# Conditions' blocks of an adaLN backbone: VectorE's running sums replaced by matmuls on four column strips of TensorE

## The chip, the cores and the metric

The kernel runs on one core of a Trainium2 chip. The metric is the device time of one execution in microseconds (us). About 0.2% of it, 6 us, can be told from no change.

## The reference

One inference step of a diffusion backbone runs four layers over 128 context tokens and 512 latent tokens of width 1024, all in fp32. The layers differ in their token mixer (SSD, gMLP, S5, neighbourhood attention), and each stands inside the same adaLN frame:

```python
cond_ctx = jax.nn.silu(c_ctx)
cond_lat = jax.nn.silu(c)[:, None, :]
for i in range(4):
    hc, gate_c = adaln(xc, norm_g[i], cond_ctx @ w_mod[i] + b_mod[i])
    hl, gate_l = adaln(xl, norm_g[i], cond_lat @ w_mod[i] + b_mod[i])
    # mixer i on hc and hl, output projection, residual with the gates
```

Only the products `cond @ w_mod[i]` matter here. There are two condition vectors of length 1024, and `w_mod[i]` is 1024 x 3072. The 3072 results (shift, scale and gate, 1024 each) are made in six blocks of 512; a block reads 1024 x 512 fp32 of `w_mod`, 2 MB, as eight k tiles of 128 rows.

## The kernel before

**Matmuls of the layers.** `Net.stream` runs all projections of a stage as one stream on TensorE. A unit is 1024 rows of weights for 128 outputs. Weights come as `raw` (512 KB, SyncE's queue, two buffers) and are split into `whi` and `wlo` (three buffers each) by ScalarE and a DMA of GpSimd's queue that adds in place (in S5's projection by GpSimd). A product is three matmuls per k tile (hi*hi, hi*lo, lo*hi), each over two halves of 320 tokens: 48 matmuls a unit. The stream is cut into slots of six matmuls, eight slots a unit, and other work is hung onto slots.

**Order.** A planner of the language arranges each engine's instructions by its own estimate of time, except on engines named in `manual_schedule`: there they stay as the program writes them. TensorE is named everywhere; VectorE, GpSimd and ScalarE only in parts (the first phase, the ends of the projections, the MLP, S5). Loads on SyncE's queue are placed by the planner, and the queue is in order: a load that waits for its buffer holds the ones behind it.

**Conditions' blocks.** The four blocks that layer 0 needs first are made at the start by `mod_pe`: per k tile one fp32 matmul with the two conditions' columns `cs[:, k, :]` as stationary operand (128 x 2) and the tile of `w_mod` as moving one (128 x 512), all into the same two rows of a PSUM bank; ScalarE copies the two rows, and four small transposes turn them so that features lie on partitions. `mod_b` then adds `b_mod` and makes the scale.

All other blocks are made by `mod_ew`, a generator that is advanced by `tick` at chosen slots of another stage: layer 0's blocks 4 and 5 in the SSD stage, layer 1's blocks 0 to 3 in SSD's output projection (`leave(0, ...)`) and 4 and 5 in the MLP, layer 2's six in the MLP's output projection, layer 3's six in S5's output projection. Each step takes two k tiles (`wm`, 512 KB): VectorE multiplies them with the condition's value on each partition and adds to `wacc` (L437 for the first k tile, L439 for the other seven, for both conditions). After four steps TensorE transposes `wacc` in eight pieces of 128 x 128 (L417), and VectorE adds up over what had been the partitions (`modq`, L418). Loads run two to three tiles ahead.

In an output projection, `use` writes each result onto the residual: `add` (VectorE, L610) and a sum of squares (`ssum`). Before it, VectorE also splits the projection's input into hi and lo (`ylo`, `gyl`, `hlo`; L205). The steps of `mod_ew` come at `MS0 + MD0 * s` (30 + 4.2 s) in SSD's projection and at `MS + MD * s` (6 + 4.6 s) in the others.

Of the kernel before, what the change touches and what calls it, by code (L numbers as in the profile page):

```python
# [7 lines left out]
F32 = mybir.dt.float32  # L8
F32R = mybir.dt.float32r
AF = mybir.ActivationFunctionType  # L10
OP = mybir.AluOpType
AX = mybir.AxisListType
# [7 lines left out]
T = TC + TL  # L20
# [7 lines left out]
SP, RM, GL = (58, 3.6), (4, 5.5), 0  # L28
MS, MD, MB = 6, 4.6, 3
# [28 lines left out]
def f(t):  # L58
    return t.bitcast(F32)
# [58 lines left out]
class Net:  # L118
# [235 lines left out]
    def cond(self):  # L354
        nc, c = self.nc, self.const
        x = c.tile([128, 8, 2], F32, name="condx")
        nc.sync.dma_start(x, self.I["cond"])
        t = c.tile([128, 8, 2], F32, name="condt")
        nc.scalar.activation(t, x, AF.Tanh, scale=0.5)
        nc.vector.tensor_scalar(t, t, 1.0, 0.5, op0=OP.add, op1=OP.mult)  # L360
        self.cs = c.tile([128, 8, 2], F32, name="conds")
        nc.vector.tensor_tensor(self.cs, x, t, op=OP.mult)

    def mod_tiles(self, i):
        c = self.const
# [1 line left out]
        self.mods[i] = (c.tile([128, 8, 2], F32, name=f"modA{i}"), m)  # L367
        return m

    def mod_w(self, i, nb, k, n, p, bufs, tag="wm"):  # L370

        w = p.tile([128, n, 512] if tag == "wm" else [128, 2, T], F32, tag=tag, bufs=bufs, name=self.n("wm"))[:, 0:n, 0:512]
        self.nc.sync.dma_start(w, self.I["w_mod"][i, nb, k // 2, :, k % 2:k % 2 + n])
        return w

    def mod_b(self, i, nb, q):
# [5 lines left out]
        if nb in (2, 3):  # L382
# [2 lines left out]
            nc.vector.scalar_tensor_tensor(a[:, s, :], m[:, 4 * nb:4 * nb + 4, :], 1.0, g[:, :, None].to_broadcast([128, 4, 2]),  # L385
                                           op0=OP.add, op1=OP.mult)

    def mod_pe(self, i, p, blocks=range(6), bufs=4, n=1):

        nc = self.nc  # L390
        for nb in blocks:
            q = self.bank("pmod")
            for k0 in range(0, 8, n):
                w = self.mod_w(i, nb, k0, n, p, bufs)
                for j in range(n):
                    k = k0 + j
                    nc.tensor.matmul(q[:2, :], self.cs[:, k, :], w[:, j, :], start=(k == 0), stop=(k == 7))
            r = p.tile([2, 512], F32, tag="modr", bufs=1, name=self.n("modr"))
            nc.scalar.copy(r, q[:2, :])
            q = self.bank("pmodt")  # L400
            for j in range(4):
                nc.tensor.transpose(q[:, 2 * j:2 * j + 2], r[:, 128 * j:128 * j + 128], self.ident[:2, :2])
            self.mod_b(i, nb, q[:, 0:8].rearrange("p (a b) -> p a b", b=2))
            yield

    def mod_ew(self, i, p, blocks=range(6), bufs=2, tags=("wm", "wacc"), pacc=None):


        nc = self.nc
        e = nc.vector  # L410

        def total(nb, acc):
            q = self.small([128, 4, 2], "modq")
            for c in range(2):
                t = self.bank("pmod")
                for j in range(4):
                    self.nc.tensor.transpose(t[:, 128 * j:128 * j + 128], acc[:, c, 128 * j:128 * j + 128], self.ident)  # L417
                e.tensor_reduce(q[:, :, c], t.rearrange("p (a b) -> p a b", a=4), axis=AX.X, op=OP.add)  # L418
            self.mod_b(i, nb, q)
        todo = [(nb, kb) for nb in blocks for kb in range(4)]  # L420
        load = lambda s: self.mod_w(i, todo[s][0], 2 * todo[s][1], 2, p, bufs, tags[0])
        ws = [load(s) for s in range(bufs - 1)]
        done = None
        for s, (nb, kb) in enumerate(todo):
            w = ws.pop(0)
            if s + bufs - 1 < len(todo):
                ws.append(load(s + bufs - 1))
            if kb == 0:
                acc = (pacc or p).tile([128, 2, 512] if tags[1] == "wacc" else [128, 2, T], F32, tag="s5gx" if pacc else tags[1],
                                       bufs=2 if pacc else 2 if tags[1] == "wacc" else bufs,  # L430
                                       name=self.n("wacc"))[:, :, 0:512]
            for j in range(2):
                k = 2 * kb + j
                for c in range(2):
                    a = self.cs[:, k, c:c + 1]
                    if k == 0:
                        e.tensor_scalar(acc[:, c], w[:, j], a, 0.0, op0=OP.mult, op1=OP.add)  # L437
                    else:
                        e.scalar_tensor_tensor(acc[:, c], w[:, j], a, acc[:, c], op0=OP.mult, op1=OP.add)  # L439
            yield  # L440
            if kb == 1 and done:
                total(*done)
            if kb == 3:
                done = nb, acc
                if pacc:
                    total(*done)
                    done = None
        if done:
            total(*done)
        yield  # L450

    def put_beside(self, *work):
# [139 lines left out]
    def leave(self, i, y, sq=None, perm=None, mod=None):  # L592


        nc = self.nc
# [3 lines left out]
        put = lambda s, g: at.setdefault(s, []).append(g)  # L599
# [5 lines left out]
        n = self.layers.index(i) + 1  # L605
# [52 lines left out]
        if i + 1 in self.layers:  # L658
            self.mod_tiles(i + 1)
            blocks = range(4 if i == 0 else 6)  # L660
            self.rest = i == 0
            self.put_beside(self.mod_ew(i + 1, self.tp, blocks, bufs=4 if mod else MB, tags=mod or ("wm", "wacc")))
            for s in range(4 * len(blocks) + 4):
                put((MS0 if i == 0 else MS) + int((MD0 if i == 0 else MD) * s), lambda: self.tick(1))
        self.wlo = nc.gpsimd
# [63 lines left out]
    def put(self, yd, k, y):  # L729

        self.nc.sync.dma_start(yd[:, 2 * k:2 * k + 2, :], y)
# [406 lines left out]
class Mlp:  # L1138
# [30 lines left out]
    def groups(self, N, h, G, tab):  # L1169
        W = N.I["w_mlp"]  # L1170
        jobs, at = [], {}
        put = lambda s, f, *a: at.setdefault(s, []).append(lambda: f(*a))
        one = lambda w, f, *a: jobs.append(([W[w]], h, 128, lambda p: f(N, *a, p)))
        for k in range(16):
            one(16 + k, self.value, G[k // 2], k)
        stats = self.stats(N)
        put(128 + 6, next, stats, None)
        put(128 + 14, next, stats, None)
        for g, P in enumerate(G):
            for j in range(2):  # L1180
                one(2 * g + j, self.input, P, "u", j, AF.Gelu_apprx_tanh)
            for j in range(2):
                one(32 + 2 * g + j, self.input, P, "z", j, AF.Silu)
            t = 128 + 32 * g
            put(t + 14, self.norm, N, P)
            put(t + 22, self.turn, N, P)
            put(t + 27, self.mix, N, P)
            for j, (a, b) in enumerate(CLOSE):
                put(t + a, self.gate, N, P, j)
                put(t + b, self.close, N, P, j)  # L1190
        for s in range(7, 128 + 32 * 8, 8):
            put(s, N.tick, 1)
        if N.rest:

            mod = []
            put(RM[0] - 1, lambda: mod.append(N.mod_ew(1, self.tp, (4, 5), MB, pacc=N.tp)))
            for k in range(10):
                put(RM[0] + int(RM[1] * k), lambda: next(mod[0], None))
        if 2 in N.layers:
            gen = tab.tables(N)  # L1200
            for k in range(90):
                put(SP[0] + int(SP[1] * k), next, gen, None)
        N.play(jobs, at, after=[N.I["w_out"][1, 0, 0]], also=(mybir.EngineType.DVE, mybir.EngineType.Pool))
# [95 lines left out]
class S5tab:  # L1299
# [49 lines left out]
    def load(self, N, tp):  # L1349
        nc, I = N.nc, N.I  # L1350
        lp = tp.tile([128, 3, 128], F32, name="lp")
        nc.sync.dma_start(lp, I["s5_lp"])
        lq = tp.tile([128, 3, 256], F32, name="lq")
        nc.sync.dma_start(lq, I["s5_lq"])
        sgn = tp.tile([128, 8], F32, name="sgn")
        nc.sync.dma_start(sgn, I["s5_sgn"])
        self.given = lp, lq, sgn
# [769 lines left out]
for _name, _w in (("b_mod", 96), ("norm_g", 32), ("final_g", 8), ("dt_bias", 1), ("a_log", 1), ("conv_w", 160),  # L2127
# [1 line left out]
                  ("s5_d", 16), ("b_glu", 16)):  # L2129
    VEC[_name] = (NVEC, _w)  # L2130
    NVEC += _w
NCONST = 664


def net(ctx, tc, I, O, layers=(0, 1, 2, 3)):
# [53 lines left out]
def layout(inp):  # L2189
    a = {k: np.asarray(v) for k, v in inp.items()}  # L2190
    x = np.concatenate([a["x_prompt"][0], a["x_sample"][0]], 0).T
    r = {"x": np.ascontiguousarray(x.reshape(8, 128, T).transpose(1, 0, 2))}
    r["cond"] = np.ascontiguousarray(np.stack([a["c_ctx"], a["c"][0]], 0).reshape(2, 8, 128).transpose(2, 1, 0))
    i = np.arange(128)
    r["consts"] = np.concatenate([i[:, None] == i, i[:, None] % 8 == i[:8],
                                  i[:, None] <= i, i[:, None] >= i, i[:, None] > i, i[:, None] < i,
                                  i[:, None] // 8 == i[:16]], 1).astype(np.float32)
    r["w_mod"] = np.ascontiguousarray(a["w_mod"].reshape(4, 4, 2, 128, 6, 512).transpose(0, 4, 1, 3, 2, 5))
    r["w_out"] = np.stack([tiles(w, 8) for w in a["w_out"]])
    w = a["ssd_w_in"][0]  # L2200
# [38 lines left out]
    c, k, rw = np.arange(16), np.arange(32), np.arange(8)  # L2239
# [10 lines left out]
    w = bias.reshape(16, 2, 128, 3, 256).transpose(0, 2, 1, 3, 4)  # L2250
# [43 lines left out]
```

## Time and profile before

| what | value |
|---|---|
| median of 3 runs | 3027.43 us (3025.84 to 3032.1) |
| the profiled execution's own time | 3024.37 us |
| its span, first to last instruction | 3022.4 us |
| busy: TensorE, VectorE, ScalarE, GpSimd | 2747.4, 2085.6, 1478.1, 1275.1 us |
| VectorE's L439, `wacc` | 280 instructions, 224.7 us |
| `w_mod` loads | 96 of 512 KB |

PE is TensorE's matmuls, PEld its weight loads, DVE VectorE, ACT ScalarE, POOL GpSimd, SP SyncE; a `q` behind the name is the engine's queue. Busy times count overlapping instructions once. An fp32 matmul leaves two records, one of the fp32r type (the layers' streams) one. A record's duration holds some 0.2 us of latency that the next one overlaps, so the rate of a stream is read from many records in a stretch, not from the mean of one.

### The profile page before, as it was taken

Reading aid. Unit: us, or ns where it says so; the run is one execution under the profiler, and the core shown is the slowest. Engines: PE = TensorE matmul, PEld = TensorE weight load, DVE = VectorE, ACT = ScalarE, POOL = GpSimd, SP = SyncE. Lnnn points to the kernel's source line nnn. Section 1 sums busy time; section 2 is a strip of 40 time slices with the busy share of each in tenths; the row PEclk is TensorE's granted clock in tenths of the full one; section 3 lists DMA queues with packets and bytes.
Section 4 is the critical chain, followed back from the end, with each engine's and each line's share of the span. In section 5 each row is a group of like instructions: output and inputs, shape, how many; then the busy total and the mean of one; then the engine's idle time right before and its main releaser. Section 6 shows DMA issues by size and latency. Waiting matters only on the chain.

```text
span 3022.4 us, 50482 instructions
## 1 busy us (share of the span) xinstructions
PE 2747.4 (91%) x18412; PEld 2636.6 (87%) x18412; DVE 2085.6 (69%) x4948; ACT 1478.1 (49%) x2525; POOL 1275.1 (42%) x1452
## 2 busy tenths in 40 slices
PE   6879989999988888989898876999899999999998
PEld 3768989899988888989898775999889999999998
DVE  5987776676679887735888972225957777777842
ACT  5534434534443444356675553444136666666641
POOL 4466667512576663123443540223343333333332
PEclk9989999999999999999898887999999999999999
DMA  7666667797676667967676569324525444444342
GB/s 254 170 182 164 174 164 192 191 288 220 172 215 194 164 194 227 278 184 219 164 221 169 147 172 186 106 92 135 202 86 148 133 135 131 136 129 135 111 181 85
DMA packets 271734, 517.91 MB, mean 171 GB/s; under 512 B 77888, under 2 KB 146944, under 8 KB 270464
## 3 DMA queue, kind: packets, MB, share of 16 engines
q1 hardware_dynamic: 240512, 411.93, 44.5%
q0 software_dynamic: 24064, 87.04, 14.9%
q10 hardware_dynamic: 6912, 15.73, 1.4%
q8 instruction: 146, 2.39, 0.3%
q14 instruction: 100, 0.82, 0.1%
HBM read 333.83 MB, written 65.70 MB: 132 GB/s over the span
## 4 chain that ended last, share of the span: by engine, by line
PE 31%; DVE 25%; DMA 13%; POOL 9%; ACT 8%; issue 7%; SPq 1%; ACTq 0%; POOLq 0%; DVEq 0%
PE acc L326 25%; DMA wlo<-raw 4%; DVE S L1771 3%; DVE wacc L439 2%; DVE sl L1768 2%; DVE e L2077 2%; DVE cacc L915 2%; POOL dd L1022 2%; POOL dd L1029 2%; ACT e L2075 1%; DMA raw<-in_w_mlp_dram 1%; DVE sb L2072 1%; DMA raw<-in_w_out_dram 1%; DVE pt L205 1%; DVE yn L2108 1%
## 5 line engine op out<-in xcount | busy, mean ns | idle before, releaser
L326 PE MATMUL acc<-hhi,whi 128*128 128x320 f32 (+2 forms) x3472 | 624.2, 319 | 25.4 <-DVE x L610 10.2
L326 PE MATMUL acc<-hlo,whi 128*128 128x320 f32 (+2 forms) x3472 | 633.0, 319 | 2.5 <-DVE hlo L579 1.3
L326 PE MATMUL acc<-hhi,wlo 128*128 128x320 f32 (+2 forms) x3472 | 613.9, 318 | 6.8 <-DMA wlo<-raw 6.8
L326 PEld LDWEIGHTS acc<-hhi,whi 128*128 128x128 f32 (+1 forms) x3472 | 542.7, 193 | 35.3 <-issue 14.6
L326 PEld LDWEIGHTS acc<-hhi,wlo 128*128 128x128 f32 (+1 forms) x3472 | 544.8, 194 | 13.2 <-DMA wlo<-raw 8.7
L326 PEld LDWEIGHTS acc<-hlo,whi 128*128 128x128 f32 (+1 forms) x3472 | 544.7, 193 | 7.9 <-DVE hlo L579 2.8
L226 POOL DMA_DIRECT2D wlo<-raw x164 | 145.1, 891 | 541.8 <-ACT wlo L225 491.9
L205 POOL TENSOR_TENSOR wlo<-raw,whi 128x1024 fp32r<-128x1024 f32 x95 | 244.6, 2576 | 262.9 <-ACT whi L204 86.7
L227 ACT CAST whi<-raw 128x1024 fp32r<-128x1024 f32 (+1 forms) x164 | 170.6, 1041 | 244.8 <-DMA raw<-in_w_mlp_dram 100.3
L225 ACT ACTIVATE wlo<-raw 128x1024 fp32r<-128x1024 f32 (+1 forms) x164 | 173.2, 1057 | 168.7 <-DMA raw<-in_w_mlp_dram 87.9
L439 DVE SCALAR_TENSOR_TENSOR wacc<-wm,conds,wacc 128x512 f32<-128x512 f32 x280 | 224.7, 855 | 30.4 <-DMA wm<-in_w_mod_dram 30.4
L326 PE MATMUL acc<-y,whi 128*128 128x320 f32 (+2 forms) x1024 | 175.8, 312 | 7.1 <-DVE y L746 3.1
L1771 DVE TENSOR_TENSOR S<-S,sl 128x32 f32<-128x32 f32 x1008 | 176.4, 230 | 0.0
L204 ACT CAST whi<-raw 128x1024 fp32r<-128x1024 f32 x125 | 129.2, 1046 | 76.0 <-PE acc L326 67.8
L326 PEld LDWEIGHTS acc<-y,whi 128*128 128x128 f32 x1024 | 155.5, 188 | 10.6 <-DVE y L746 4.5
L2077 DVE TENSOR_SCALAR e<-e,mx 128x384 f32<-128x384 f32 (+1 forms) x160 | 154.1, 963 | 4.2
L915 DVE SCALAR_TENSOR_TENSOR cacc<-pad,vec,cacc 128x644 f32<-128x644 f32 x128 | 144.2, 1127 | 2.2 <-ACT cacc L913 0.9
L2075 ACT ACTIVATE e<-sb,mx 128x384 f32<-128x384 f32 x128 | 79.0, 617 | 107.3 <-DVE mx L2074 106.6
L1768 DVE TENSOR_TENSOR sl<-S,A 128x64 f32<-128x64 f32 x504 | 120.9, 280 | 0.0
L1889 DVE TENSOR_TENSOR y<-y,sg 128x640 f32<-128x640 f32 x16 | 14.1, 879 | 150.2 <-ACT sg L1888 150.2
L1547 POOL TENSOR_TENSOR s5gy<-Bu,Qt 128x512 f32<-128x512 f32 x64 | 90.0, 1438 | 57.3 <-DVE s5gx L1557 53.9
L1022 POOL TENSOR_TENSOR dd<-cmat,dt 128x512 f32<-128x512 f32 x80 | 108.2, 1358 | 12.2 <-DVE dt L826 9.4
(407 smaller groups left out, 5381.9 us busy)
## 6 DMA issues: line engine op xcount, KB each, us to landing
wlo<-raw POOLq DMA_DIRECT2D x163, 512.0 KB, 5.4
wm<-in_w_mod_dram SPq DMA_DIRECT2D x96, 512.0 KB, 6.5
raw<-in_w_out_dram SPq DMA_DIRECT2D x64, 512.0 KB, 4.5
raw<-in_w_nat_dram SPq DMA_DIRECT2D x64, 512.0 KB, 3.8
raw<-in_w_ssd_dram SPq DMA_DIRECT2D x48, 512.0 KB, 3.5
raw<-in_w_mlp_dram SPq DMA_DIRECT2D x48, 512.0 KB, 3.6
fb<-fd SPq DMA_DIRECT2D x40, 512.0 KB, 5.4
s5X<-s5gx SPq DMA_DIRECT2D x32, 512.0 KB, 4.8
```

The lines of the kernel that those rows point to most:

```text
L204: (hi_eng or nc.scalar.copy)(hi, src)
L205: (lo_eng or nc.vector).tensor_tensor(lo, src, f(hi), op=OP.subtract)
L225: self.nc.scalar.activation(lo, raw, AF.Copy, scale=-1.0)
L226: self.nc.gpsimd.dma_start(lo, raw, accum_op=OP.add)
L227: self.nc.scalar.copy(hi, raw)
L326: mm(p[:m, o:o + c], w[:, kt, :], v(hx), start=(k == 0 and wi == 0), stop=(k == 8 * len(units) - 1 and wi == 2))
L439: e.scalar_tensor_tensor(acc[:, c], w[:, j], a, acc[:, c], op0=OP.mult, op1=OP.add)
L915: nc.vector.scalar_tensor_tensor(acc, pad[:, j:j + 644], w(j), acc, op0=OP.mult, op1=OP.add)
L1022: nc.gpsimd.tensor_tensor(dg.rearrange("p (h l) -> p h l", h=4), N.ident[:, None, :].to_broadcast([128, 4, 128]), self.dt[:, c, 32 * d + 4 ...
L1768: e.tensor_tensor(t[d], F[:, d, at[d], None, :].to_broadcast([128, 2, 32]), A[:, :, d], op=OP.mult)
L1771: e.tensor_tensor(dst[d], dst[d], t[d][:, k].rearrange("p (r g) -> p r g", r=2)[:, ::1 - 2 * k], op=OP.add)
L2077: nc.vector.tensor_scalar(e[:, :w], e[:, :w], m[:, 3:4], None, op0=OP.mult)
```

## The change

The eight matmuls of a block are spread over four groups of 32 columns of TensorE: k tile k writes to PSUM partitions 32 (k mod 4) to 32 (k mod 4) + 31, so that four partial sums stand beside each other. The stationary operand is 32 columns wide, starting at the two columns of k (the 30 others are neighbours or zeros and are not used). ScalarE copies the whole bank (128 x 512), and four fp32 matmuls with `sel` (128 x 2, ones where the partition is 0 or 1 modulo 32) add the four partial sums and turn them in one step. `mod_pe` and `mod_ew` both use it; `wacc`, VectorE's sums, the transposes and `modq` go. `mod_ew` is still advanced in four steps per block: all four loads of a block at once, the end of the block before in the second step, the matmuls in the fourth, and then the next block's loads. Buffers: four `wm` tiles instead of two or three and two `wacc`; where only three fit, the fourth is lent by another tag.

```diff
@@ cond
+        self.csx = c.tile([128, 48], F32, name="condsx")
+        nc.vector.memset(self.csx, 0.0)
+        nc.vector.tensor_copy(self.csx[:, 0:16], self.cs.rearrange("p k c -> p (k c)"))
+        self.sel = c.tile([128, 2], F32, name="sel")
+        nc.sync.dma_start(self.sel, self.I["consts"][:, 664:666])
@@ new
+    def mod_sums(self, ws):
+        q = self.bank("pmod")
+        for k, w in enumerate(ws):
+            o = 32 * (k % 4)
+            self.nc.tensor.matmul(q[o:o + 32, :], self.csx[:, 2 * k:2 * k + 32], w, start=(k < 4), stop=(k >= 4))
+        return q
+
+    def mod_end(self, i, nb, r):
+        q = self.bank("pmodt")
+        for j in range(4):
+            self.nc.tensor.matmul(q[:, 2 * j:2 * j + 2], r[:, 128 * j:128 * j + 128], self.sel, start=True, stop=True)
+        self.mod_b(i, nb, q[:, 0:8].rearrange("p (a b) -> p a b", b=2))
@@ mod_pe
+            ws = [self.mod_w(i, nb, k, n, p, bufs) for k in range(0, 8, n)]
+            q = self.mod_sums([w[:, j, :] for w in ws for j in range(n)])
+            r = p.tile([128, 512], F32, tag="modr", bufs=1, name=self.n("modr"))
+            self.nc.scalar.copy(r, q)
+            self.mod_end(i, nb, r)
@@ mod_ew, in place of VectorE's sums
+        lend = lambda: more[0].tile([128, 2, 512], F32, tag=more[1], bufs=2, name=self.n("wm"))
+        load = lambda nb: [self.mod_w(i, nb, 2 * kb, 2, p, MB if more else 4, tags[0], lend if more and kb == 3 else None)
+                           for kb in range(4)]
+        blocks = list(blocks)
+        ws, done = load(blocks[0]), None
+        for n, nb in enumerate(blocks):
             yield
+            if done:
+                self.mod_end(i, *done)
+                done = None
+            yield
+            yield
+            q = self.mod_sums([w[:, j, :] for w in ws for j in range(2)])
...
+            self.nc.scalar.copy(r, q)
+            done = nb, r
+            if n + 1 < len(blocks):
+                ws = load(blocks[n + 1])
+            yield
+        self.mod_end(i, *done)
         yield
@@ leave
-            self.put_beside(self.mod_ew(i + 1, self.tp, blocks, bufs=4 if mod else MB, tags=mod or ("wm", "wacc")))
+            self.put_beside(self.mod_ew(i + 1, self.tp, blocks, tags=mod or ("wm", "modr"), more=(self.tp, "wacc") if i == 1 else None))
@@ groups (the MLP)
-            put(RM[0] - 1, lambda: mod.append(N.mod_ew(1, self.tp, (4, 5), MB, pacc=N.tp)))
+            put(RM[0] - 1, lambda: mod.append(N.mod_ew(1, self.tp, (4, 5), more=(N.tp, "s5gx"))))
@@ constants
-NCONST = 664
+NCONST = 666
```

## Rows read from the trace of the kernel before

**Rows 1.** The page: head, and shares of the chain that ended last, by engine.

```profile
PE 2747.4 (91%) x18412; PEld 2636.6 (87%) x18412; DVE 2085.6 (69%) x4948; ACT 1478.1 (49%) x2525; POOL 1275.1 (42%) x1452
...
PE 31%; DVE 25%; DMA 13%; POOL 9%; ACT 8%; issue 7%; SPq 1%; ACTq 0%; POOLq 0%; DVEq 0%
```

**Rows 2.** Windows of tile `wacc`: length, busy by engine (instructions), clock, DMA, GB/s.

```profile
60.00:200.00 140.00, 0.00 (x0) 0.00 (x0) 29.31 (x32) 0.90 0.65 172
630.00:710.00 80.00, 4.42 (x32) 3.63 (x32) 42.13 (x64) 1.00 0.94 273
735.00:800.00 65.00, 2.35 (x16) 1.77 (x16) 23.21 (x32) 0.95 0.83 229
1175.00:1300.00 125.00, 6.21 (x48) 5.60 (x48) 64.57 (x96) 0.99 0.88 258
2090.00:2200.00 110.00, 4.77 (x32) 4.44 (x32) 86.06 (x96) 0.95 0.56 188
```

**Rows 3.** Windows of all engines, same columns.

```profile
150.00:180.00 30.00, 20.50 (x123) 18.75 (x124) 30.00 (x30) 11.77 (x18) 18.54 (x14) 0.85 0.66 189
630.00:660.00 30.00, 30.00 (x209) 30.00 (x209) 21.25 (x35) 8.12 (x10) 2.59 (x3) 1.00 1.00 310
750.00:780.00 30.00, 29.63 (x204) 29.31 (x204) 26.03 (x38) 13.43 (x19) 9.51 (x7) 1.00 0.85 234
1230.00:1260.00 30.00, 30.00 (x211) 29.98 (x210) 24.28 (x41) 9.41 (x10) 2.64 (x3) 1.00 0.94 271
2125.60:2187.60 62.00, 62.00 (x416) 61.85 (x416) 62.00 (x83) 9.75 (x11) 27.55 (x7) 0.96 0.62 213
```

**Rows 4.** TensorE's waits, 60 to 200 us: for whom, us, times, longest.

```profile
PE G L1054 <- DVE xw L1047: 7.9, 2, 7.3
PE stc L1077 <- DVE xw L1047: 7.1, 1, 7.1
...
PE acc L326 <- DVE hlo L205: 0.5, 1, 0.5
```

**Rows 5.** TensorE's waits, 2090 to 2225 us.

```profile
PE acc L326 <- DVE x L610: 10.2, 3, 6.6
```

**Rows 6.** TensorE's waits, 1175 to 1305 us.

```profile
PE acc L326 <- DVE ylo L205: 2.5, 2, 2.2
```

**Rows 7.** Timeline of TensorE, 33 to 41 us: start us, us, what.

```profile
33.44 7.03 PE L397 MATMUL pmod<-wm,conds 128*2 128x512 f32 x16
```

**Rows 8.** Timeline of TensorE, 212 to 216 us.

```profile
212.30 0.39 PE L1054 MATMUL G<-c,b 128*128 128x128 f32 x2
...
215.25 0.66 PE L1068 MATMUL yd<-dd,xb 128*64 128x128 f32 x8
```

**Rows 9.** Timeline of TensorE, 215.2 to 215.3 us.

```profile
215.25 0.33 PE L1068 MATMUL yd<-dd,xb 128*64 128x128 f32 x2
```

**Rows 10.** Timeline of TensorE's weight loads, 215 to 216.2 us.

```profile
215.25 0.42 PEld L1068 LDWEIGHTS yd<-dd,xb 128*64 128x64 f32 x8 [0.19 <-issue]
```

**Rows 11.** Timeline of TensorE, 655 to 670 us.

```profile
662.17 1.04 PE L417 MATMUL pmod<-cmat,wacc 128*128 128x128 f32 x8
```

**Rows 12.** Timeline of TensorE, 0 to 75 us.

```profile
30.27 1.28 PE L469 MATMUL cols<-ones,ssum 128*128 128x1 f32 x10
```

**Rows 13.** Timeline of ScalarE, 40 to 59 us.

```profile
54.88 1.06 ACT L225 ACTIVATE wlo<-raw 128x1024 fp32r<-128x1024 f32 x1 [11.34 <-DMA raw<-in_w_ssd_dram]
...
56.77 0.57 ACT L399 COPY modr<-pmod 2x512 f32<-2x512 f32 x1
```

**Rows 14.** TensorE's waits, 600 to 735 us.

```profile
PE pmod L417 <- DVE wacc L439: 0.7, 1, 0.7
```

**Rows 15.** Timeline of TensorE, 2190 to 2200 us.

```profile
2190.65 3.77 PE L326 MATMUL acc<-hhi,whi 128*128 128x320 f32 x16 [2.87 <-DVE x L610]
...
2196.95 2.51 PE L326 MATMUL acc<-hhi,wlo 128*128 128x320 f32 x16
```

**Rows 16.** VectorE's waits, 600 to 760 us.

```profile
DVE wacc L439 <- DMA wm<-in_w_mod_dram: 10.5, 6, 3.9
```

More of the change, by code (lines that the diff above doesn't have):

```diff
@@ L368, in mod_tiles, with mod_w @@
         return m
-    def mod_w(self, i, nb, k, n, p, bufs, tag="wm"):
-        w = p.tile([128, n, 512] if tag == "wm" else [128, 2, T], F32, tag=tag, bufs=bufs, name=self.n("wm"))[:, 0:n, 0:512]
+    def mod_w(self, i, nb, k, n, p, bufs, tag="wm", lend=None):
+        w = lend() if lend else p.tile([128, n, 512] if tag == "wm" else [128, 2, T], F32, tag=tag, bufs=bufs, name=self.n("wm"))
+        w = w[:, 0:n, 0:512]
         self.nc.sync.dma_start(w, self.I["w_mod"][i, nb, k // 2, :, k % 2:k % 2 + n])
@@ L388, in mod_pe @@
     def mod_pe(self, i, p, blocks=range(6), bufs=4, n=1):
-        nc = self.nc
         for nb in blocks:
[L392 to L403, printed above, removed]
-            yield
@@ L406, in mod_ew @@
[L406 to L439, printed above, removed]
-            yield
[L441 to L449, printed above, removed]
@@ new lines, in mod_pe, with mod_ew @@
+            ws = [self.mod_w(i, nb, k, n, p, bufs) for k in range(0, 8, n)]
[3 more added lines that the diff above has]
+            self.mod_end(i, nb, r)
+            yield
+    def mod_ew(self, i, p, blocks=range(6), tags=("wm", "modr"), more=None):
+        lend = lambda: more[0].tile([128, 2, 512], F32, tag=more[1], bufs=2, name=self.n("wm"))
[4 more added lines that the diff above has]
+        for n, nb in enumerate(blocks):
+            yield
+            if done:
[4 more added lines that the diff above has]
+            q = self.mod_sums([w[:, j, :] for w in ws for j in range(2)])
+            if more:
+                r = lend()[:, 0]
+            elif tags[1] == "modr":
+                r = p.tile([128, 512], F32, tag="modr", bufs=1, name=self.n("modr"))
+            else:
+                r = p.tile([128, 2, T], F32, tag=tags[1], bufs=4, name=self.n("modr"))[:, 0, 0:512]
+            self.nc.scalar.copy(r, q)
[4 more added lines that the diff above has]
+        self.mod_end(i, *done)
@@ L2196, in layout @@
                                   i[:, None] <= i, i[:, None] >= i, i[:, None] > i, i[:, None] < i,
-                                  i[:, None] // 8 == i[:16]], 1).astype(np.float32)
+                                  i[:, None] // 8 == i[:16], i[:, None] % 32 == i[:2]], 1).astype(np.float32)
     r["w_mod"] = np.ascontiguousarray(a["w_mod"].reshape(4, 4, 2, 128, 6, 512).transpose(0, 4, 1, 3, 2, 5))
```

## The prediction

> **What bounds the kernel now.** The head of the page comes first: TensorE is busy for 91% of the span and VectorE for 69%, yet the chain that ended last gives TensorE 31% and VectorE 25% [rows 1]. So no engine bounds the whole kernel, and what VectorE's sums cost has to be read stage by stage. The windows of the tile `wacc` say where they stand: 29.3 us of VectorE at the start of the SSD stage, 42.1 in SSD's output projection, 23.2 at the start of the MLP, 64.6 in the MLP's projection, 86.1 in S5's projection [rows 2]; 32 instructions are two blocks, so there are 20 blocks.
>
> Next, the busy windows of all engines in the same places show which of these VectorE us are in anybody's way [rows 3]. Where TensorE does only its 320-column matmuls it fits 209 to 211 records into 30 us (630 to 660, 1230 to 1260). There VectorE is busy for 21 to 24 us of 30 and holds nobody up; any work put on TensorE lengthens the stage by its own length. 750 to 780 is nearly such a place (204). It is otherwise at 150 to 180: 123 records, VectorE busy for all 30.0. In S5's projection VectorE is busy for all 62.0 us of the window, while TensorE keeps its rate between waits.
>
> The waits confirm it. From 60 to 200 us, eight kinds of TensorE's waits end on VectorE, from 7.9 us for `xw` down to 0.5 for `hlo`, 26.3 us together [rows 4]. In S5's projection it waits 10.2 us for `x`, the residual update behind the sums in VectorE's queue [rows 5]; in the MLP's, 2.5 us for `ylo` [rows 6].
>
> **The sums on TensorE.** A block's eight fp32 matmuls are 16 records, which took 7.03 us in the first layer, 0.43 each [rows 7]. This is what they cost one after another. The change gives four of them different 32-column strips. No row has four strips, but `yd` has two: it alternates between two strips of 64. Eight of its records, 128 columns each, took 0.66 us from first start to last end, while two records of the untiled `G`, same shape, took 0.39 [rows 8]. With 0.27 us of latency in each, that is 0.12 a record untiled and 0.055 in two strips: the strips run beside each other. The first two `yd` records both start within 50 ns [rows 9], so records of different strips pair up from the first. I take four strips as four times: 7.03 / 4 = 1.76 us. The weight load of `yd` sits idle for 0.19 us at the change of strip width [rows 10], and there is a change back: 0.25 us for both. So 2.0 us a block. The other ends are 3.7 (pairs only) and 7.1 (no overlap).
>
> The Trainium skill, TensorEngine Tiling, Key Properties, says that changing the tiling mode drains TensorE, which speaks against short tiled groups in a dense stream; the 0.19 us agrees, and at twice a block it changes the sum by the 0.25 already in it.
>
> The end of a block stays equal. Eight transposes of 128 x 128 took 1.04 us [rows 11]; now four fp32 matmuls of 128 x 2 run, eight records, nearest to `cols`, ten records in 1.28 us [rows 12], so 1.0 us. ScalarE gets a 128 x 512 copy per block, nearest the 2 x 512 copy of 0.57 us; it is busy for 8 to 9 of 30 us in the projections [rows 3], which hides it. The number of `w_mod` loads stays the same; one small load, of `sel`, joins SyncE's queue at the start.
>
> **Stage by stage.**
>
> Start (0 to 60 us): the first four blocks become 5 us shorter each on TensorE. But block 3's end waits for ScalarE's copy at 56.77, which stands behind two conversions whose raw weights came at 54.88 [rows 13]. The weights' buffer is what is late, not the sums: 0. If ScalarE's order comes out otherwise, at most the 11.3 us that it waited for those weights are saved; if the added small copies and the DMA of `sel` tell, +1. Range -11 to +1.
>
> SSD start: VectorE loses 29.3 us, in a stretch where TensorE waits some 26 us for VectorE. Neither end is likely: VectorE also waits there for a DMA and GpSimd, and those chains stay. I take half, -14.6, and +4.0 for two blocks on TensorE, whose order is fixed as written: -10.6. Range -25 (all returns) to +4 (none).
>
> SSD's projection: 4 blocks x 2.0 = 8.0 on a full TensorE, less a wait of 0.7 for `wacc` there [rows 14]: +7.3. MLP start: two blocks, 4.0, nearly all visible: +3.5. MLP's projection: 6 x 2.0 = 12.0, less the 2.5 us wait: +9.5.
>
> S5's projection: back come the 10.2 us of waits, and slow clock behind them. TensorE restarted at 2190.65 with 16 records in 3.77 us against 2.51 a little later [rows 15]; the window before has a granted clock of 0.96 over 62 us, that is 5 us at 1.2 instead of 2.4 GHz, 2.5 us lost. With 1.4 for the restart at 2190, 14.1 returns; 12.0 is added: -2.1. Range -8 (the projection also gets shorter waits elsewhere) to +8 (VectorE's freedom gives back a third).
>
> Waits for `w_mod`: until now a late tile stopped VectorE (10.5 us in SSD's projection [rows 16]) and not TensorE. Now the sums stand in TensorE's written order, and a late tile stops the stream; all four loads of the next block are issued only after the sums of this one, and SyncE's loads of `w_out` queue behind them. Between two blocks' sums lie 17 or 18 slots of six matmuls, 0.86 us each by the 209 records in 30 us, so 15 us, for 2 MB; the DMA is at 1.00 there and moves 310 GB/s for all [rows 3], so half of that rate would do it in 13 us. Tight, not short: +3 us over the three projections, range 0 to +20.
>
> Sum: 0 - 10.6 + 7.3 + 3.5 + 9.5 - 2.1 + 3 = +10.6 us. The profiled execution took 3024.37 us, 2 us more than its span, and lies 3 us under the median of 3027.43; the sum, made on the trace, is carried to the median: 3038.
>
> **Rivals.**
>
> A, faster: the SSD start returns everything. Place: 60 to 200 us; price: 29.3 instead of 14.6 us, and with prompt loads (no +3) the sum becomes -7, so 3020. For it: VectorE has no idle time at all from 150 to 180. Against: the waits on `fb` and GpSimd. It decides once more than 25 of the 29.3 us return. Chance 0.23.
>
> B, the strips overlap only in pairs. Each fp32 matmul is two records on the same strip; if TensorE starts records strictly in program order, the second must wait for the first, and the next strip can start only then. A block then costs 3.7 us, 1.7 more, on 18 blocks that lie beside full TensorE or fill it: +31, so 3069. Against it stand the first two `yd` records, which start together, where such an order would start the second a whole record later. No overlap at all would be 5 us more on 20 blocks, some 3135. Chance 0.13, with 0.02 of it for the last. The Trainium skill, TensorE: Matmul & The Clock Gate, part 3, states that matmuls start and end in strict program order; by that rule B would be the outcome, and `yd` doesn't bear it out for two strips.
>
> C, the wait for `w_mod` takes the place of the one removed: late tiles stop TensorE for about 1.25 us in each of the projections' 16 blocks: +20 instead of +3, so 3055. For it: the DMA at 1.00 and VectorE's 10.5 us; against: a slower TensorE stream also asks for fewer weights a microsecond. Chance 0.19.
>
> The forecast itself: 0.45.
>
> **How the numbers follow.** About 0.2% (6 us) is what a measurement of this kernel tells from no change. The likeliest case gives 3038, its own range 3028 to 3050 from half of the SSD range and half of the S5 range. Slower by over 0.2%, above 3033.5: three quarters of the forecast's 0.45, all of B and C: 0.66, of which I give 0.07 back for the planner, which orders the engines anew and may do so better. Faster, under 3021.4: most of A and some of that: 0.22. Within: the rest, 0.19. For the range, A's lower half (0.08) is left out below 3017, and half of B (0.08) above 3070.
>
> **What would show it.** `pmod` matmuls with 16 records in about 2.0 us, four starting together, confirm the strips; 3.5 us is B. From 60 to 200 us, `wacc` gone and waits for `xw` cut to half is the forecast; gone altogether is A. In the projections of SSD and the MLP, TensorE's stage gets longer by 7 to 10 us with the record rate unchanged; waits of `pmod` for `w_mod` over 1 us each are C. In S5's projection, the three waits [rows 5] vanish and the stage keeps its length. The step that I trust least is the half at the SSD start, then the 3 us of waits; wrong strips would make all other terms small.

## The result and the profile after

The changed kernel took 3050.7 us (median of four runs, 3048.85 to 3056.26) against 3028.52 for the kernel before on the same chip (four runs, 3025.84 to 3032.10). The ratio is 1.0071, 95% interval 1.0058 to 1.0084, so it is slower by 22 us (18 to 25). Slower was forecast, with 3038 and a range of 3017 to 3070; the loss is twice the 10.6 us of the sum, and 3050.7 lies just above the likeliest case's own range of 3028 to 3050.

The page of the profile after, head and chain (compare [rows 1]):

```profile
span 3054.5 us, 50800 instructions
...
PE 2781.9 (91%) x18748; PEld 2651.1 (87%) x18748; DVE 1832.3 (60%) x4590; ACT 1487.4 (49%) x2543; POOL 1246.1 (41%) x1452
...
PE 39%; DVE 22%; DMA 10%; ACT 8%; POOL 7%; issue 5%; SPq 1%; ACTq 0%; POOLq 0%; DVEq 0%
```

VectorE lost 253 us of work and the kernel got slower: most of that work stood in nobody's way. TensorE got 34 us more, and its share of the chain rose from 31% to 39%.

TensorE's timeline from 640 us, in SSD's projection, and the same cut short at 640.55 (start us, us, what):

```profile
640.50 1.93 PE L400 MATMUL pmod<-wm,condsx 128*32 128x512 f32 x16
```

```profile
640.50 0.64 PE L400 MATMUL pmod<-wm,condsx 128*32 128x512 f32 x4
```

A block is 16 records in 1.93 us, where [rows 7] had 7.03; four of them have started within 50 ns. This is the 2.0 us a block of the prediction.

TensorE's waits from 60 to 200 us (compare [rows 4]), and then in S5's projection, 2120 to 2255 us (compare [rows 5]):

```profile
PE stc L1074 <- DVE xw L1044: 4.7, 2, 3.3
PE G L1051 <- DVE dd L1054: 4.0, 1, 4.0
...
PE st L1074 <- DVE xw L1044: 1.3, 1, 1.3
PE G L1051 <- DVE xw L1044: 0.5, 1, 0.5
```

```profile
PE acc L326 <- DVE x L607: 0.8, 1, 0.8
```

The waits for `xw` fell from 15.0 us and more to 6.5, and one for `dd` came up instead. In S5's projection 10.2 us became 0.8.

Windows of all engines where TensorE is full, and 150 to 180 us, where VectorE held it up before (compare [rows 3]; length, busy by engine with instructions, granted clock, DMA, GB/s):

```profile
630.00:660.00 30.00, 30.00 (x215) 26.99 (x213) 5.50 (x9) 10.85 (x12) 3.48 (x4) 1.00 0.87 234
150.00:180.00 30.00, 30.00 (x215) 28.41 (x214) 20.60 (x24) 14.86 (x24) 18.89 (x18) 1.00 0.60 155
1260.00:1290.00 30.00, 30.00 (x213) 28.37 (x212) 4.15 (x10) 8.78 (x11) 2.61 (x3) 1.00 0.92 256
2155.00:2217.00 62.00, 62.00 (x439) 56.08 (x441) 8.59 (x15) 12.37 (x14) 16.86 (x8) 1.00 0.60 191
```

In the three projections VectorE dropped from between 21 and 62 us busy to under 9, and TensorE is as full as before: these stages can only get longer, by the blocks. From 150 to 180 us TensorE now has 215 records where it had 123.

To see where the 22 us arose, the traces were laid beside the first profile of the kernel before: each instruction of ScalarE and VectorE that occurs equally often in both (the conditions' own left out) was compared with the same occurrence by its start, and the median offset was taken at the ends of the stages. What the offset gains from one end to the next is the table; columns are the ends of the stages in us of the first profile, and all kernels of the experiments are in it. Each row is one execution, and executions differ: the changed kernel's took 3056.26 us, 6 over its median, and the first profile of before 3024.37, 4 under that of before, so the first row adds up to 32 us and not to 22.

```
                        58  355  605  735  935 1174 1324 1775 1925 2288  end
changed kernel        -5.3 -7.3  1.3  9.3 13.3  0.9  8.1  2.0  8.2  2.1 -0.6
before, again          1.0 -1.7 -0.7  0.6  4.1  0.1 -3.0  2.2  0.6  1.2  0.2
before, shifted        0.1 -4.1  2.3  1.1  4.4  0.5 -1.9  3.3  5.9 -1.0  0.2
14 more columns       -5.4 -7.0  0.9  7.1 13.8  1.9  8.2  5.4  6.5  2.0 -0.1
change in place       -4.8 -8.2  0.9  7.3 12.3  2.3  6.6  3.3  3.6  1.7 -0.4
ScalarE's order       -5.4-10.1 -1.6  8.3  4.6  4.6  6.9  4.7  6.5  1.0 -2.6
in place and order    -5.0 -8.9  2.8  7.3  5.0  3.1  6.6  4.9  2.8  1.9 -2.7
not the MLP's start   -4.8 -6.3  2.6  7.1  3.5  1.5  8.6  7.1  9.1  2.3 -0.1
first and SSD start   -4.7-11.0 -1.4  0.0 10.1  4.4 -0.3  3.0  7.9  2.7  0.4
 and S5's projection  -4.6 -7.2  1.6  0.2  8.0  2.7  0.3  5.8  7.7 -0.6  1.4
first and SSD, place  -5.0 -8.7 -0.4 -0.1  6.0  2.4 -0.1  2.6  5.1 -0.6  1.8
 and S5's, in place   -5.6-12.7 -1.4  0.7  4.1  1.9 -3.7  2.9  0.9  1.0  2.2
one strip              0.4 -7.9 -1.8 28.8 17.3  2.4 40.0  0.5  8.6 31.2  0.0
```

Two columns of the first row stand out: 13.3 us at the MLP's start (up to 935), where 3.5 were forecast, and 8.2 at the end of the S5 stage (1775 to 1925), where no instruction came or went. The experiments are about these.

TensorE's waits from 738 to 925 us, before and after (for whom, us, times, longest):

```profile
PE acc L326 <- DMA wlo<-raw: 5.7, 6, 2.5
```

```profile
PE acc L326 <- DMA wlo<-raw: 13.7, 5, 4.7
```

ScalarE's timeline of the changed kernel there, from 784 us (start us, us, what, idle before and releaser), and GpSimd's:

```profile
784.56 1.06 ACT L225 ACTIVATE wlo<-raw 128x1024 fp32r<-128x1024 f32 x1 [4.41 <-DMA raw<-in_w_mlp_dram]
785.53 1.03 ACT L227 CAST whi<-raw 128x1024 fp32r<-128x1024 f32 x1
786.46 0.58 ACT L441 COPY wm<-pmod 128x512 f32<-128x512 f32 x1
790.91 1.05 ACT L227 CAST whi<-raw 128x1024 fp32r<-128x1024 f32 x1 [3.87 <-DMA raw<-in_w_mlp_dram]
791.86 0.70 ACT L1206 ACTIVATE y<-acc 128x640 f32<-128x640 f32 x1
792.46 1.05 ACT L225 ACTIVATE wlo<-raw 128x1024 fp32r<-128x1024 f32 x1
793.40 0.73 ACT L1213 ACTIVATE sq<-y 128x640 f32<-128x640 f32 x1
```

```profile
781.82 0.87 POOL L226 DMA_DIRECT2D wlo<-raw  x1
794.29 1.57 POOL L1214 TENSOR_TENSOR ssum<-ssum,sq 128x640 f32<-128x640 f32 x1 [11.60 <-ACT sq L1213]
795.81 0.87 POOL L226 DMA_DIRECT2D wlo<-raw  x1
```

Read it as a chain. At 784.56 and 785.53 ScalarE starts to write `wlo` and `whi` of one unit. The planner now puts the next unit's `whi` ahead of this unit's `y` and `sq`; it waits 3.87 us for raw weights, and everything behind it waits too. `sq` comes at 793.40, GpSimd's `ssum` stands behind `sq`, and the accumulating DMA that finishes `wlo` stands behind `ssum` in GpSimd's queue: it is issued at 795.81, though `wlo` was written by 785.6. The raw buffer comes free later still, so the next load and TensorE's next units are late.

### The profile page after: what moved, and what is told of

It reads as the page before. It is cut to its first block, busy times and chain, and to the rows that moved or that the text cites. A ratio compares the mean times of both kernels' runs of the same rounds, so it can differ in the third digit from the quotient of the medians.

```text
span 3054.5 us, 50800 instructions
## 1 busy us (share of the span) xinstructions
PE 2781.9 (91%) x18748; PEld 2651.1 (87%) x18748; DVE 1832.3 (60%) x4590; ACT 1487.4 (49%) x2543; POOL 1246.1 (41%) x1452
## 3 DMA queue, kind: packets, MB, share of 16 engines
q0 software_dynamic: 24064, 87.04, 15.2%
## 4 chain that ended last, share of the span: by engine, by line
PE 39%; DVE 22%; DMA 10%; ACT 8%; POOL 7%; issue 5%; SPq 1%; ACTq 0%; POOLq 0%; DVEq 0%
PE acc L326 31%; DVE S L1768 3%; DMA wlo<-raw 3%; DVE sl L1765 2%; DVE e L2074 2%; DMA raw<-in_w_mlp_dram 2%; DVE cacc L912 2%; ACT e L2072 1%; POOL dd L1019 1%; DVE sb L2069 1%; DVE yn L2105 1%; POOL dd L1026 1%; DVE pt L205 1%; ACT zr L1611 1%; PE S L2063 1%
## 5 line engine op out<-in xcount | busy, mean ns | idle before, releaser
L205 POOL TENSOR_TENSOR wlo<-raw,whi 128x1024 fp32r<-128x1024 f32 x95 | 230.1, 2422 | 274.6 <-PE acc L326 105.8
L326 PEld LDWEIGHTS acc<-y,whi 128*128 128x128 f32 x1024 | 156.5, 189 | 12.7 <-DVE y L205 4.1
L607 DVE SCALAR_TENSOR_TENSOR x<-acc,mod,x 128x128 f32<-128x128 f32 (+3 forms) x53 | 29.3, 595 | 224.0 <-PE acc L326 222.6
L2105 DVE TENSOR_TENSOR yn<-yn,av 64x128 f32<-64x128 f32 x320 | 90.6, 283 | 32.4 <-ACT yn L2103 23.6
```

The source lines that it names most:

```text
L205: (lo_eng or nc.vector).tensor_tensor(lo, src, f(hi), op=OP.subtract)
L326: mm(p[:m, o:o + c], w[:, kt, :], v(hx), start=(k == 0 and wi == 0), stop=(k == 8 * len(units) - 1 and wi == 2))
L2105: nc.vector.tensor_tensor(y[r, o], y[r, o], p[r, w:w + 128], op=OP.add)
```

## The experiments

Ten kernels were run 5 to 12 times each; two, the kernel before itself and the one with one strip, once. Times are medians, with the kernel before on the same chip. Single runs of the kernel before spread from 3014 to 3041 us over these sessions, so only ratios with their intervals count.

**ScalarE's order at the MLP's start.**

```
+        act = ExitStack()
+        put(3, lambda: act.enter_context(N.tc.manual_schedule(engines={mybir.EngineType.Activation})))
+        put(57, act.close)
```

> The changed kernel, but at the MLP's start (slots 3 to 57 of its stream) ScalarE takes its work in the order in which it is written (lo half, hi half, y, square), as the planner had it before the change. Theory (the planner's new order, in which a conversion that waits for late weights stands ahead of y and its square, delays the next weights' loads and so TensorE): about 8 us return, +14 us against the kernel before instead of +22; the waits of TensorE for wlo from 755 to 930 fall from 13.7 us to about 6. Rival (the eight w_mod loads that now come in bursts of four are what delays the weights): nothing returns, +22 us, the waits stay above 12 us.

Measured: 3041.2 against 3031.34, ratio 1.0037 (1.0023 to 1.0052): 11 us slower by the ratio, instead of 22. The MLP's start is at +4.6 in the table, and the wait from 738 to 925 us in this kernel is back at

```profile
PE acc L326 <- DMA wlo<-raw: 7.1, 4, 3.3
```

with all 20 blocks still on TensorE. The order it is, and not the bursts of `w_mod` loads, which stayed: SyncE's queue issues four in a row in both traces.

**Two blocks less: the MLP's start on VectorE as before** (`N.mod_ve`, the old `mod_ew`, for blocks 4 and 5 of layer 1).

> The changed kernel, but the two blocks at the MLP's start are summed on VectorE as before. Theory (these two blocks cost 13 us in the profile, 4 of them TensorE's own work): +10 us against the kernel before. Rival (they cost their TensorE time only, and what else was lost from 755 to 930 is another matter): +18 us.

Measured: 3042.86, ratio 1.0042 (1.0025 to 1.0058), 13 us slower: nearer to the theory, and the rival's 18 is just outside the interval. The MLP's start is at +3.5. As the kernel before repeated has +4.1 there, the two blocks cost about 9 us in the changed kernel and next to nothing with ScalarE's order written out. Its row in the table is of an execution of 3055.1 us, the longest of the five.

**Only the first four blocks and the SSD start**; the other 18 blocks by the old `mod_ew`; and the same with S5's projection on TensorE as well.

> TensorE's sums for the first four blocks and the two blocks at the start of the SSD stage alone; the other 18 blocks on VectorE as before. Theory (the gain made there, 4 us in the first 60 us and 6 to 12 at the SSD start, stays to the end): -10 us against the kernel before, range -7 to -14. Rival (it is given back at a later wait): within 3 us of the kernel before.

> As the run with the first blocks and the SSD start alone, and S5's projection too on TensorE (12 of 24 blocks). Theory (there 14 us of waits return and 12 us of TensorE's time are added): the same as that run within 3 us, about -10 us against the kernel before. Rival (the 8 us that the changed kernel's profile shows in the S5 stage between 1780 and 1880 come with the change): 6 to 10 us more than that run, some -2 us.

Measured: 3035.17, ratio 1.0011 (0.9996 to 1.0026), and 3034.8, ratio 1.0019 (1.0006 to 1.0032). The theory fell: 16 us are gained up to 355 us in the one and 12 in the other, as the table shows, and all is gone at the end. The losses lie in stages that these kernels don't change, and every kernel with the change's tiles has about the same loss at the end of the S5 stage. Their largest loss, 10.1 and 8.0, is at the MLP's start, where they have neither the two blocks on TensorE nor the changed order of ScalarE. Either the first profile of before was quick there, or something shared slows them.

**The kernel before, again; and with its buffers shifted.**

```
+        pad = c.tile([128, 50], F32, name="condpad")
+        nc.vector.memset(pad, 0.0)
```

> The kernel before, once more with a profile, since in all five profiles with TensorE's sums the MLP's start (755 to 925) and the S5 stage (1325 to 1900) come out 4 to 13 and 10 to 15 us longer than in the first profile of the kernel before, also where nothing was changed in them. Theory A (these stages wait for transfers whose time differs from execution to execution, and the first profile of before was a quick one): this profile has them 5 to 12 us longer in sum than the first. Theory B (something that all five kernels share makes these stages slower): this profile has them as the first, within 3 us.

> The kernel before with 50 more unused columns (200 bytes a partition, as much as the change's two small constant tiles) in the pool of constants, so that every later buffer lies 200 bytes further on. Theory B, in the form that the shift of the buffers is what all five kernels share: 8 to 12 us slower than the kernel before, in the MLP's start and the S5 stage. Theory A: no change, within 3 us.

The repeated kernel ran in 3028.92 us. Its profile has 4.1 us more at the MLP's start and 2.8 more in the S5 stage than the first: 4 us at the MLP's start can be the spread of executions. The shifted kernel took 3036.11 against 3029.25, ratio 1.0024 (1.0013 to 1.0036): 7 us slower. In the built program each engine has the same instructions in the same order as before, but for that memset, and the same waits, but for one that moved between two loads of `x`. So both theories hold, each for its part, and this shift of the buffers costs 7 us (4 to 11). The end of the S5 stage is at +5.9.

**Another shift.**

```
-        self.csx = c.tile([128, 48], F32, name="condsx")
+        self.csx = c.tile([128, 62], F32, name="condsx")
```

> The changed kernel with 14 more unused columns in its constant tile, so that all later buffers lie 256 bytes instead of 200 further on than before. Theory B (the odd shift slows transfers): some 10 us return, +12 us against the kernel before. Theory A: +22 us as the changed kernel, within 4 us.

Measured: 3052.23, ratio 1.0066 (1.0043 to 1.0089): nothing returned. The run didn't test what it was meant to. In the built program tiles are placed in steps of 32 bytes; `wlo` and `raw` lie on multiples of 256 bytes in the kernel before, 160 bytes past one in the changed kernel, and 224 past one here and in the shifted kernel. No multiple was restored. These places are the built programs'; the traces hold no addresses.

**One strip for all eight k tiles.**

```
-            o = 32 * (k % 4)
+            o = 0
...
-            self.nc.tensor.matmul(q[o:o + 32, :], self.csx[:, 2 * k:2 * k + 32], w, start=(k < 4), stop=(k >= 4))
+            self.nc.tensor.matmul(q[o:o + 32, :], self.csx[:, 2 * k:2 * k + 32], w, start=(k == 0), stop=(k == 7))
```

ScalarE's copy and the four matmuls of `mod_end` take these 32 rows alone.

> The changed kernel with all eight k tiles of a block on the same 32 columns, one after another, so that the sums are the same and no strips lie beside each other. By the trace of the kernel before (0.43 us a record): 7 us a block instead of 2, so +100 us on the 20 blocks that were on VectorE, some 3145 us; the first four blocks longer too, where they are not waiting for data. If the strips gave nothing, the time would stay at 3050.

Measured: 3143.64 us in one run, +93 over the changed kernel, as expected. TensorE's timeline of this kernel from 640 us:

```profile
641.49 7.05 PE L400 MATMUL pmod<-wm,condsx 128*32 128x512 f32 x16
...
664.80 7.05 PE L400 MATMUL pmod<-wm,condsx 128*32 128x512 f32 x16
```

In the table the projections are 19.5, 31.9 and 29.1 us longer than in the changed kernel: 4.9, 5.3 and 4.9 us a block, the 5.1 us between 7.05 and 1.93. There nearly all of TensorE's time is visible.

**The conditions packed in place.** The three small tiles of the conditions (192 bytes) become one, which also serves as `csx` and `sel`:

```
+        self.csx = c.tile([128, 48], F32, name="conds")
+        x, t = (self.csx[:, o:o + 16].rearrange("p (k c) -> p k c", c=2) for o in (0, 16))
+        self.sel = self.csx[:, 46:48]
...
+        nc.vector.tensor_tensor(x, x, t, op=OP.mult)
+        nc.vector.memset(self.csx[:, 16:32], 0.0)
```

> The whole changed kernel, but its padded conditions and its selector lie in the 192 bytes a partition that the three small tiles of the conditions took before. In the built program the later buffers then lie on multiples of 64 bytes again, as in the kernel before; in the changed kernel, in all runs so far that carry its two tiles and in the shifted kernel before they lie 32 bytes beside such multiples (the run with 14 more columns left that so). Theory (the place of the buffers costs 7 us, above all at the end of the S5 stage): +15 us against the kernel before, range +11 to +18, and the S5 stage from 1775 to 1925 within 3 us of the kernel before instead of 6 to 9 above. Rival (the place matters in the kernel before only by chance): +22 us.

> TensorE's sums for the first four blocks and the two at the SSD start alone, with the conditions packed in place, so that no buffer moves. Theory (12 us gained up to 355 us, nothing lost later): -10 us against the kernel before, range -6 to -14. Rival (the gain is given back, as in the run with the moved buffers, whatever the place): +3 us.

> As the run with the first blocks and the SSD start in place, and S5's projection on TensorE too. Theory (its price and its gain there are equal): within 3 us of that run, so -10 us against the kernel before. Rival (the forecast of -2 for this projection): 2 us less than that run; or the 1 to 2 us more that the changed kernel's profiles show there.

Measured: the whole change in place 3042.53 against 3030.31, ratio 1.0045 (1.0030 to 1.0060), +14 us; the first blocks and the SSD start in place 3026.08, ratio 0.9986 (0.9971 to 1.0001), -4 us; with S5's projection 3024.62, ratio 0.9981 (0.9967 to 0.9996), -6 us. The first lies between its theory (-10) and its rival (+3). The last kernel is ahead of the kernel before, barely clear of noise and not by the 10 us expected; the two part kernels lie within 3 us of each other, as expected. Against their twins with moved buffers they are 0.25 and 0.38% faster, 8 and 11 us, by ratios taken in different sessions; the intervals of the first pair overlap a little, those of the second are apart. Together with the shifted kernel's 7 that is three pairs that differ in the place and in little else (in two of them the conditions are also packed otherwise at the start).

The queue of the accumulating `wlo` transfers, from the pages of four kernels (packets, MB, time as a share of 16 engines' span): before again, before shifted, the first blocks and the SSD start with moved buffers and in place.

```profile
span 3026.9 us, 50482 instructions
...
q0 software_dynamic: 24064, 87.04, 15.0%
```

```profile
span 3033.3 us, 50483 instructions
...
q0 software_dynamic: 24064, 87.04, 15.4%
```

```profile
span 3033.5 us, 50545 instructions
...
q0 software_dynamic: 24064, 87.04, 15.5%
```

```profile
span 3025.3 us, 50545 instructions
...
q0 software_dynamic: 24064, 87.04, 14.9%
```

Span times share is 454, 467, 470 and 451 us of 16 engines for the same packets. Over all profiles but the one-strip kernel's it is 450 to 454 in the four with unmoved buffers and 464 to 470 in the nine with moved ones. The rounding of the share is worth 1.5 us; even so the five that lie 224 bytes past a multiple of 256, by the tiles that each kernel has, are the highest (467 to 470, against 464 to 466 for the four at 160 and 192). The whole change in place belongs to the nine (466 us): as the old sums' small tiles `modq` are gone too, its buffers lie 64 bytes lower than before, on multiples of 64 but not of 256. So the +14 came as its theory had it, without the theory's condition; it can still hold some of the price of the place, and why its end came out 8 us lower than the changed kernel's, with the same transfer time, stays open; the intervals of the two ratios touch.

**Both unforeseen costs taken out.**

> The whole change with both unforeseen costs taken out: the conditions packed in place (as in the run of that name) and ScalarE's work at the MLP's start in its written order (as in the first run). Theory (they are separate, 8 and 9 us): +22 - 8 - 9 = +5 us against the kernel before, range +2 to +9. Rival (they overlap, both being late transfers at the MLP's start): +10 to +14 us.

Measured: 3038.35 against 3028.97, ratio 1.0036 (1.0017 to 1.0056), +9 to +11 us: at the edge of either theory. In its profile both stages are where the theory wants them (+5.0 at the MLP's start, +2.8 at the end of S5), but that execution took 3042.31 us, with +2.8, +3.1 and +4.9 in stages that the two edits don't touch. Whether the two costs add up, or one hides part of the other, stays open at this spread. Two comparisons speak against full prices for both: with ScalarE's order written out, the kernels with moved and with packed conditions are alike (1.0037 and 1.0036; neither has its buffers on multiples of 256), and with packed conditions the order gives back 3 us by the ratios (1.0045 and 1.0036, with intervals that overlap widely).

## Why the prediction was right, and where its terms were off

The sign was right, for the reason given: VectorE's time has no price where TensorE is full, and TensorE's has. The size was not: 3050.7 is nearer to rival C's 3055 than to the forecast's 3038, and C's cause did not occur, so the time alone would have picked the wrong story. Term by term, forecast against the table:

- **Strips.** 2.0 us a block forecast, 1.93 measured. Rival B is out. The Trainium skill, TensorE: Matmul & The Clock Gate, part 3, has matmuls start and end in strict program order. With a matmul's two records one behind the other, as the prediction took them, four records that start within 50 ns, and 1.93 us instead of 7.05 with the strips taken away, don't agree with it where the strips differ; in which order the program lists the records no trace shows.
- **Start.** 0 forecast (-11 to +1), -5.3 measured. The chance named there came true: the planner put ScalarE's copy for block 3 at 43.09 us, ahead of the conversions that it stood behind in [rows 13]. With one strip nothing is gained here (+0.4), so the strips are needed too.

```profile
43.09 0.59 ACT L416 COPY modr<-pmod 128x512 f32<-128x512 f32 x1 [3.62 <-PE pmod L400]
```

- **SSD start.** -10.6 forecast; -7.3 up to 355 us, and -6.3 to -12.7 in all eleven kernels with it, where the kernel before repeated has -1.7 and the shifted one -4.1. Rival A is out. Half was about right from 60 to 200 us, where TensorE's waits for VectorE fell from 26.3 us to 13.0. Behind 200 us `pmod` and `pmodt` each wait over 5 us for `dd`, whose PSUM bank they take over; in the kernel before, `xbT` waited 7.2 us for `dd` there, so 3.4 of these 10.6 us are more than before. With 3.9 us for the two blocks that makes -6.0, near the table's -7.3 against -1.7. The waits of the changed kernel, then of the kernel before, 200 to 345 us:

```profile
PE pmodt L407 <- DVE dd L1054: 5.5, 1, 5.5
PE pmod L400 <- DVE dd L1054: 5.1, 1, 5.1
```

```profile
PE xbT L1043 <- DVE dd L1057: 7.2, 2, 3.8
```

  The windows 205 to 215 us of the two part kernels in place show what came with such a wait: after one of 5.1 us the granted clock is 0.78, after one of 2.9 it is 1.00. The kernel before lost clock there too: 0.86 and 0.80 in its two windows from 215 to 235 us, around the first wait of `xbT`.

```profile
205.00:215.00 10.00, 10.00 (x64) 7.21 (x56) 7.05 (x10) 5.08 (x9) 5.56 (x6) 0.78 0.86 309
```

```profile
205.00:215.00 10.00, 8.73 (x61) 8.06 (x61) 7.88 (x12) 4.99 (x9) 7.08 (x7) 1.00 0.85 311
```

- **SSD's projection.** +7.3 and a share of the 3 us for waits forecast; +7.1 to +9.3 in six kernels with the blocks there, -0.1 to +1.1 in six without.
- **MLP's projection.** +9.5 forecast; +6.6 to +8.6 in those six, -3.7 to +0.3 in the others. Right.
- **S5's projection.** -2.1 forecast; -0.6 to +2.3 in the eight kernels (one strip left out) with TensorE's sums, -1.0 to +2.7 in the four with VectorE's. The waits all but vanished as forecast (0.8 us is left), and the stage kept its length. The restart that the sum has at 1.4 us is 1.3 by [rows 15].
- **Waits for `w_mod`.** +3 forecast; behind the SSD start `pmod` waited 0.2 us for a load and its weight loads 1.4. Rival C is out: the loads come in time.
- **MLP start.** +3.5 forecast, +13.3 measured, of which the repeated kernel has 4. This is the step that failed: "two blocks, 4.0, nearly all visible". The two blocks were priced as TensorE's time in a full stream, and the order that the planner makes of the engines was only given chances, on the side of a gain. It cost 8 to 9 us here; shown by the run with ScalarE's order written out, in its time (+11 instead of +22) and in the waits (7.1 instead of 13.7 us). The size is less sure than the cause: single profiles of kernels with neither the blocks nor the new order have +3.5 to +10.1 in this stage.
- **Place of the buffers.** Not in the sum. The words "one small load, of `sel`, joins SyncE's queue" price the two small tiles by their instructions; they also moved every buffer behind them. Some 7 us for a shift of 224 bytes, shown by the shifted kernel before and supported by the two part kernels; how much the changed kernel's 160 bytes cost was not measured by itself.

Worked out from the table, rounded and against the rows that lack the part in question: -5 at the start, -6 for the SSD start, +8 for SSD's projection, +9 for the MLP's start, +9 for its projection, +6 for the end of S5 and +1 for S5's projection are +22, the measured difference. That they meet so well is in part the choice of rows: against the repeated kernel alone the same seven terms come to +26. Of the forecast's terms those for the start (-5), the SSD start (+5), S5's projection (+3) and the waits (-3) were off and cancelled, which is luck; 5.5 us more at the MLP's start and 6 at the end of S5 are what was missing between 10.6 and 22.

## What to carry to other kernels

Price work by the stage it stands in: moving 20 blocks off an engine that was busy for 69% of the span lost in the stages where TensorE is full, came out even in S5's projection, and was worth it only for the two blocks where TensorE waited for VectorE, with the first four: some 4 us in that kernel, 6 with S5's projection, at the edge of what can be told from no change. When an edit adds or removes loads and conversions beside a planner, compare the order of every engine before and after; one conversion that waits for its data in front of three that don't can cost more than the edit's own work, here 8 to 9 us against 4. Keep small new tiles from moving the large ones, or test the kernel before with the same shift, before a loss is put down to the edit.

## What the runs showed of the hardware

A shift of all large buffers by 160 to 224 bytes from multiples of 256 made the same 24064 packets of the accumulating queue take 464 to 470 us of engine time instead of 450 to 454, and one such shift, of 224 bytes, made the kernel before 7 us longer. The Trainium skill, DMA: Bandwidth & Descriptors, How a descriptor splits into AXI transactions, says that a descriptor which doesn't start on a multiple of 256 bytes first fetches from the boundary below it and pays for the bytes that it doesn't use. By its beats a run of 4096 bytes, the size of most of these packets in the trace, would take 133 to 135 beats instead of 128, 4 to 5.5% more, an estimate from that page; the 3% measured agrees in sign and about in size. That this is how the 7 us arise is not shown, since the loss lies mostly at the end of the S5 stage, where most of the transfers are others.

Four fp32 matmuls on four 32-column strips of TensorE run fully beside each other: 16 records of 512 columns took 1.93 us instead of 7.05.
